# Retention heads of a hybrid encoder block: one transpose for the keys of two heads, and one instruction for the decayed keys

## The chip, the cores and the metric

The kernel runs on one core of a Trainium2 chip. The metric is device time in microseconds of one execution, the median of the runs shown. The engines are TensorE (PE for its matmuls, PEld for its weight loads), VectorE (DVE), ScalarE (ACT), GpSimd (POOL) and SyncE (SP, which only starts transfers here).

## The reference, cut to what matters

One layer: a norm and modulation of x (1024 tokens by 1024 columns), one wide input projection, a retention branch of 8 heads and a latent-attention branch of 8 heads, and an output projection. The change lies in the retention branch. There q and k (64 columns per head) get a rotary embedding, and each direction works in chunks of 128 tokens:

```
scores = einsum('bhnik,bhnjk->bhnij', qc, kc) * decay_intra
intra  = einsum('bhnij,bhnjv->bhniv', scores, vc)
kv_chunk = einsum('bhnjk,bhnjv->bhnkv', kc * k_decay, vc)
state' = state * chunk_decay + kv_chunk
cross  = einsum('bhnik,bhnkv->bhniv', qc * q_decay, states)
```

The output is intra + cross, forward with the diagonal and backward without it, summed.

## The kernel before, in words

Everything is float32. The large projections are made of three products of rounded halves (wh, wl, hh, hl), which is why lines 65 to 67 (the helper mm3) hold most of the matmuls. Weights come in pages (wpage, line 86, loaded by SP), which ACT rounds (line 80) and POOL subtracts (line 81).

The retention stage is a loop over four groups g of two heads. Within a group it runs over eight chunks t of 128 tokens. For each chunk: 24 matmuls project q, k and v into a PSUM bank of the tag acc (four banks; the tag sm has the other four). For group 0 these projections are already done. ACT copies v (line 345). DVE multiplies q and k by cosine and sine (lines 354 and 356), POOL subtracts and adds into the even slots of a buffer of eight slots of 64 columns (lines 360 and 361): q of head 0, q of head 1, k of head 0 and k of head 1 in slots 0, 2, 4 and 6. DVE copies the two q into slots 1 and 3 (line 362). Slots 5 and 7 hold zeros that line 328 put there once. DVE makes the decayed keys kd with four small instructions (line 366), one per head and direction. TensorE transposes the buffer in four blocks of 128 columns (line 370): q0 q0, q1 q1, k0 and zeros, k1 and zeros. ACT copies all four blocks to qkT (line 372), DVE makes the decayed q (line 374), TensorE the scores of both heads (line 378, where the zero half silences the second copy of q), DVE the masked scores (line 380), and TensorE the products of kd and v (line 385), which go into the states ST (lines 389 to 399).

After its eight chunks a group computes its output gates sg (line 414), the outputs in two halves (lines 424 and 425), their norm (lines 430 to 437), transposes (line 442) and the product ro (line 444), which SP writes to memory (line 446). After the four groups, mla_gate runs for two groups of gates of the other branch (line 460). Its results stand in buffers of the tag qkT until ACT's queue has written them to memory (line 461).

The order on each engine is not that of the text. A planner with a cost model orders the instructions of each engine ahead of the run, so the matmuls of lines 65 to 67 of the group's gates and of the next group stand between the small matmuls of a chunk. On the chip each engine then takes its instructions in that fixed order.

Of the kernel before, what the change touches and what calls it, by code (L numbers as in the profile page):

```python
# [9 lines left out]
F32 = mybir.dt.float32  # L10
# [3 lines left out]
ALU = mybir.AluOpType  # L14
# [4 lines left out]
P = 128  # L19
# [11 lines left out]
def body(tc, I, O):  # L31
# [292 lines left out]
    mgD = dram.tile([H, P, S], F32, name="mgD")  # L324

    rbuf = [p_ret.tile([P, 8, 64], F32, name=f"rb{i}", tag=f"rb{i}") for i in range(2)]
    for b_ in rbuf:
        G.memset(b_, 0.0)

    for g in range(4):  # L330
        w = w0 if g == 0 else [wpage(I["w_ret"][g][j], 1024, 2) for j in range(4)]
        vv = []
        ST = p_ret.tile([P, NT, 2, P], F32, name="ST", tag="ST")
        sT = [None] * NT
        qdT = [None] * NT
        for t in range(NT):
            if g == 0 and t < NB0:
                ps = acc0[t]
            else:
                ps = acc()  # L340
                for k in range(KT):
                    wh, wl = w[k // 2]
                    mm3(ps, hh[k][:, ts_(t)], hl[k][:, ts_(t)], wh[:, k % 2], wl[:, k % 2], k == 0, k == KT - 1)
            v_ = p_ret.tile([P, 2, P], F32, name="v", tag="v", bufs=9)
            A.copy(out=v_.rearrange("p h d -> p (h d)"), in_=ps[:, 256:512])  # L345
            vv.append(v_)
            xq = ps[:, 0:256]
            if g == 0 and NACC <= t < NB0:
                xq = p_ret.tile([P, 256], F32, name="xq", tag="o", bufs=5)
                A.copy(out=xq, in_=ps[:, 0:256])  # L350
            xq = xq.rearrange("p (a d) -> p a d", d=32)
            t1 = p_ret.tile([P, 4, 2, 32], F32, name="t1", tag="t1", bufs=2)
            t2 = p_ret.tile([P, 4, 2, 32], F32, name="t2", tag="t2", bufs=2)
            V.tensor_tensor(out=t1.rearrange("p a b d -> p (a b) d"), in0=xq,
                            in1=Cr[:, t:t + 1].broadcast_to([P, 8, 32]), op=ALU.mult)
            V.tensor_tensor(out=t2.rearrange("p a b d -> p (a b) d"), in0=xq,
                            in1=Sr[:, t:t + 1].broadcast_to([P, 8, 32]), op=ALU.mult)
            r_ = rbuf[t % 2]
            rv = r_.rearrange("p (a z) d -> p a z d", z=2)[:, :, 0].rearrange("p a (b d) -> p a b d", b=2)
            G.tensor_tensor(out=rv[:, :, 0], in0=t1[:, :, 0], in1=t2[:, :, 1], op=ALU.subtract)  # L360
            G.tensor_tensor(out=rv[:, :, 1], in0=t1[:, :, 1], in1=t2[:, :, 0], op=ALU.add)
            V.tensor_copy(out=r_[:, 1:4:2], in_=r_[:, 0:4:2])
            kd = p_ret.tile([P, 2, 2, 64], F32, name="kd", tag="kd", bufs=2)
            for h in range(2):
                for d in range(2):
                    V.tensor_scalar(out=kd[:, h, d], in0=r_[:, 4 + 2 * h],
                                    scalar1=kfac[:, 2 * g + h, d:d + 1], scalar2=None, op0=ALU.mult)
            tp = sm(512)
            for a in range(4):
                T.transpose(tp[:, ts_(a)], r_[:, 2 * a:2 * a + 2].rearrange("p a b -> p (a b)"), ident)  # L370
            qkT_ = p_ret.tile([P, 4, P], F32, name="qkT", tag="qkT", bufs=2)
            A.copy(out=qkT_.rearrange("p a b -> p (a b)"), in_=tp)
            qdT_ = p_ret.tile([P, 2, P], F32, name="qdT", tag="qdT", bufs=8)
            V.tensor_tensor(out=qdT_, in0=tp[:, 0:256].rearrange("p (a b) -> p a b", a=2),
                            in1=qfac[:, 2 * g:2 * g + 2], op=ALU.mult)
            scp = sm(256)
            for h in range(2):
                T.matmul(scp[:, ts_(h)], qkT_[:, 2 + h], qkT_[:, h], start=True, stop=True)
            sT_ = p_ret.tile([P, 2, P], F32, name="sT", tag="sT", bufs=8)
            V.tensor_tensor(out=sT_, in0=scp.rearrange("p (h d) -> p h d", h=2), in1=mask[:, 2 * g:2 * g + 2],  # L380
                            op=ALU.mult)
            sT[t], qdT[t] = sT_, qdT_
            kv = sm(256)
            for h in range(2):
                T.matmul(kv[:, ts_(h)], kd[:, h].rearrange("p a b -> p (a b)"), v_[:, h], start=True, stop=True)
            kvv = kv.rearrange("p (h d) -> p h d", h=2)
            if t < NT - 1:
                if t == 0:
                    V.tensor_copy(out=ST[0:64, 1], in_=kvv[0:64])
                else:  # L390
                    for h in range(2):
                        V.scalar_tensor_tensor(out=ST[0:64, t + 1, h], in0=ST[0:64, t, h],
                                               scalar=gch[0:64, 2 * g + h:2 * g + h + 1], in1=kvv[0:64, h],
                                               op0=ALU.mult, op1=ALU.add)
            if t > 0:
                A.copy(out=ST[64:128, t - 1], in_=kvv[64:128])
        for t in range(NT - 2, 0, -1):
            for h in range(2):
                V.scalar_tensor_tensor(out=ST[64:128, t - 1, h], in0=ST[64:128, t, h],
                                       scalar=gch[64:128, 2 * g + h:2 * g + h + 1], in1=ST[64:128, t - 1, h],  # L400
                                       op0=ALU.mult, op1=ALU.add)


        wg = [wpage(I["w_rg"][g][j], 1024, 4) for j in range(2)]
        sg = p_ret.tile([P, 2, S], F32, name="sg", tag="sg")
        for h in range(2):
            for half in range(2):
                ps = acc()
                for k in range(KT):
                    wh, wl = wg[k // 4]  # L410
                    rh = hh[k][:, half * 512:half * 512 + 512]
                    rl = hl[k][:, half * 512:half * 512 + 512]
                    mm3(ps, wh[:, k % 4, ts_(h)], wl[:, k % 4, ts_(h)], rh, rl, k == 0, k == KT - 1)
                A.activation(sg[:, h, half * 512:half * 512 + 512], ps, AF.Silu)

        for half in range(2):
            mv = p_ret.tile([P, 4, 2, 2], F32, name="mv", tag="mv", bufs=2)
            ob = []
            for q in range(4):
                t = half * 4 + q  # L420
                op = sm(256)
                lo, hi = (64, 128) if t == 0 else (0, 64) if t == NT - 1 else (0, 128)
                for h in range(2):
                    T.matmul(op[:, ts_(h)], sT[t][:, h], vv[t][:, h], start=True, stop=False)  # L424
                    T.matmul(op[:, ts_(h)], qdT[t][lo:hi, h], ST[lo:hi, t, h], start=False, stop=True)  # L425
                o_ = p_ret.tile([P, 2, P], F32, name="o", tag="o", bufs=5)
                A.copy(out=o_.rearrange("p h d -> p (h d)"), in_=op)
                for h in range(2):
                    bs = p_ret.tile([P, 6], F32, name="bs", tag="bs", bufs=4)
                    V.bn_stats(out=bs, in_=o_[:, h])  # L430
                    V.bn_aggr(out=mv[:, q, h], in_=bs)
                ob.append(o_)
            rst = p_ret.tile([P, 4, 2], F32, name="rst", tag="rst", bufs=2)
            rstd(rst.rearrange("p a b -> p (a b)"), mv[:, :, :, 1].rearrange("p a b -> p (a b)"), 8)
            for q in range(4):
                for h in range(2):
                    V.tensor_scalar(out=ob[q][:, h], in0=ob[q][:, h], scalar1=mv[:, q, h, 0:1],
                                    scalar2=rst[:, q, h:h + 1], op0=ALU.subtract, op1=ALU.mult)
            for h in range(2):
                tp = sm()  # L440
                for q in range(4):
                    T.transpose(tp[:, ts_(q)], ob[q][:, h], ident)
                ro = p_ret.tile([P, 512], F32, name="ro", tag="ro", bufs=2)
                V.scalar_tensor_tensor(out=ro, in0=tp, scalar=gnw[:, 2 * g + h:2 * g + h + 1],
                                       in1=sg[:, h, half * 512:half * 512 + 512], op0=ALU.mult, op1=ALU.mult)
                SY.dma_start(out=retD[2 * g + h, :, half * 512:half * 512 + 512], in_=ro)
# [14 lines left out]
                A.dma_start(out=mgD[2 * n + h, :, sl], in_=mo)  # L461

    for n in range(MG0):
        mla_gate(n, p_ret, "qkT")
    rts.close()


# [498 lines left out]
```

## Time and profile before

| | |
|---|---|
| median of 3 runs | 1058.83 us (1058.5 to 1059.71) |
| profiled execution, its time | 1057.49 us |
| its span, from the first to the last instruction | 1055.3 us |
| mean granted clock of TensorE | 0.988 of full speed |

The span is what the views of the trace divide up. The profiled execution lies 1.34 us under the median, so differences are taken within the trace and then applied to the median.

### The profile page before, as it was taken

The numbers are of one execution on the slowest core, as the hardware profiler recorded it, in microseconds if no ns is written. First come the engines' busy times: TensorE is split into PE (matmuls) and PEld (weight loads), VectorE is DVE, ScalarE is ACT, GpSimd is POOL, SyncE is SP. The second block draws the span as 40 slices with busy tenths as digits, with TensorE's granted clock in tenths as the row PEclk, the third lists the DMA queues.
The fourth block names the chain that finished last, engine by engine and source line by source line (L and its number), as shares of the span: only waits on it lengthen the run. The fifth ranks groups of instructions, "written<-read, shape, count | busy, mean of one in ns | idle before, by whom it ended". The sixth has DMA issues, their size and how long they took to land.

```text
span 1055.3 us, 15223 instructions
## 1 busy us (share of the span) xinstructions
PE 1018.1 (96%) x5736; PEld 888.3 (84%) x5736; DVE 581.4 (55%) x1390; ACT 426.0 (40%) x800; POOL 404.1 (38%) x311
## 2 busy tenths in 40 slices
PE   5899999999999999999999999989999999989998
PEld 4687887888888888998888889879889999878887
DVE  7996546444643534336302116777877777883342
ACT  6654213312321322124322006577767776772100
POOL 2233315213411411224633217943466555873210
PEclk8899999999999999999999999999999999998999
DMA  9721103101110212224654520100000000003522
GB/s 365 264 64 57 41 1 120 41 2 62 63 36 20 85 47 73 102 84 136 201 171 153 183 85 11 41 1 2 20 21 21 2 20 22 21 20 120 169 101 70
DMA packets 30744, 82.27 MB, mean 78 GB/s; under 512 B 3536, under 2 KB 4560, under 8 KB 30672
## 3 DMA queue, kind: packets, MB, share of 16 engines
q1 hardware_dynamic: 25920, 72.92, 20.4%
q10 hardware_dynamic: 4752, 8.39, 2.2%
q8 instruction: 45, 0.74, 0.3%
q14 instruction: 27, 0.22, 0.1%
HBM read 64.52 MB, written 16.78 MB: 77 GB/s over the span
## 4 chain that ended last, share of the span: by engine, by line
PE 82%; DVE 11%; DMA 2%; ACT 2%; issue 2%; POOL 2%; ACTq 0%; DVEq 0%; POOLq 0%
PE acc L65 13%; PE acc L66 13%; PE acc L67 13%; PE pt L739 4%; PE sp L65 4%; PE sp L66 4%; PE sp L67 4%; PE po L66 3%; PE po L67 3%; PE po L65 3%; DVE x L178 2%; DMA wa<-w_ada 2%; PE sm L425 2%; PE sm L424 1%; PE sm L65 1%
## 5 line engine op out<-in xcount | busy, mean ns | idle before, releaser
L81 POOL TENSOR_TENSOR wl<-wr,wh 128x1024 fp32r<-128x1024 f32 (+2 forms) x51 | 115.2, 2268 | 173.2 <-ACT wh L80 148.9
L65 PE MATMUL acc<-wh,hh 128*128 128x512 f32 (+2 forms) x352 | 130.8, 372 | 1.7 <-ACT hh L189 1.7
L66 PE MATMUL acc<-wl,hh 128*128 128x512 f32 (+2 forms) x352 | 130.3, 370 | 0.0
L67 PE MATMUL acc<-wh,hl 128*128 128x512 f32 (+2 forms) x352 | 126.4, 368 | 2.1 <-DVE hl L190 2.1
L725 POOL TENSOR_SCALAR pr<-pr,st 128x1024 f32<-128x1024 f32 x62 | 72.0, 1165 | 101.1 <-DVE st L724 75.5
L65 PE MATMUL acc<-hh,wh 128*128 128x512 f32 x256 | 101.0, 395 | 1.7 <-ACT v L345 1.7
L742 DVE TENSOR_TENSOR pl<-pt,ph 128x512 fp32r<-128x512 f32 x128 | 85.3, 683 | 31.2 <-ACT ph L741 31.1
L66 PE MATMUL acc<-hl,wh 128*128 128x512 f32 x256 | 100.9, 394 | 0.0
L67 PE MATMUL acc<-hh,wl 128*128 128x512 f32 x256 | 100.6, 393 | 0.0
L80 ACT CAST wh<-wr 128x1024 fp32r<-128x1024 f32 (+2 forms) x55 | 53.8, 982 | 104.1 <-PE sm L66 45.1
L741 ACT CAST ph<-pt 128x512 fp32r<-128x512 f32 x128 | 73.1, 591 | 26.6 <-PE pt L739 24.6
L720 DVE TENSOR_REDUCE st<-sp 128x1 f32<-128x1024 f32 x62 | 75.4, 1216 | 6.5 <-PE sp L67 6.4
L66 PE MATMUL po<-pl,vh 128*128 128x256 f32 x256 | 76.5, 299 | 2.1 <-DVE pl L742 2.0
L723 ACT ACTIVATE pr<-sp,st 128x1024 f32<-128x1024 f32 x62 | 69.5, 1121 | 20.8 <-DVE st L721 20.5
L65 PEld LDWEIGHTS acc<-wh,hh 128*128 128x128 f32 x352 | 67.2, 191 | 10.9 <-ACT hh L189 2.1
L67 PEld LDWEIGHTS acc<-wh,hl 128*128 128x128 f32 x352 | 66.0, 188 | 11.1 <-DVE hl L190 3.0
L66 PEld LDWEIGHTS acc<-wl,hh 128*128 128x128 f32 x352 | 67.3, 191 | 8.7
L739 PE MATMUL pt<-ident,pr 128*128 128x128 f32 x496 | 70.2, 274 | 4.0 <-DVE st L724 2.7
L65 PE MATMUL po<-ph,vh 128*128 128x256 f32 x256 | 73.3, 286 | 0.0
L67 PE MATMUL po<-ph,vl 128*128 128x256 f32 x256 | 72.8, 284 | 0.0
L360 POOL TENSOR_TENSOR rb<-t,t 128x128 f32<-128x128 f32 x32 | 14.8, 464 | 135.0 <-PE sm L370 73.4
L739 PEld LDWEIGHTS pt<-ident,pr 128*128 128x128 f32 x496 | 57.9, 141 | 8.5 <-issue 2.9
(353 smaller groups left out, 2474.2 us busy)
## 6 DMA issues: line engine op xcount, KB each, us to landing
x<-w_ada SPq DMA_DIRECT2D x16, 512.0 KB, 7.1
wr<-w_ret SPq DMA_DIRECT2D x16, 512.0 KB, 3.5
wr<-w_rg SPq DMA_DIRECT2D x8, 512.0 KB, 3.5
retD<-ro SPq DMA_DIRECT2D x16, 256.0 KB, 2.1
wr<-w_mg SPq DMA_DIRECT2D x8, 512.0 KB, 3.5
wa<-w_ada SPq DMA_DIRECT2D x8, 512.0 KB, 3.5
wr<-w_out SPq DMA_DIRECT2D x8, 512.0 KB, 4.5
wro<-retD SPq DMA_DIRECT2D x8, 512.0 KB, 3.9
```

The lines of the kernel that those rows point to most:

```text
L65: T.matmul(out, lh, rh, start=first, stop=False, **kw)
L66: T.matmul(out, lh, rl, start=False, stop=False, **kw)
L67: T.matmul(out, ll, rh, start=False, stop=last, **kw)
L80: A.copy(out=hi, in_=raw)
L81: eng.tensor_tensor(out=lo, in0=raw, in1=hi, op=ALU.subtract)
L178: V.scalar_tensor_tensor(out=wa, in0=wa, scalar=1.0, in1=sc, op0=ALU.mult, op1=ALU.mult, accum_out=mp[:, i:i + 1])
L720: V.tensor_reduce(out=st_[:, 0:1], in_=sp, op=ALU.max, axis=AX.X)
L723: A.activation(pr, sp, AF.Exp, bias=st_[:, 1:2], scale=sc_, accum_out=st_[:, 2:3])
L725: G.tensor_scalar(out=pr, in0=pr, scalar1=st_[:, 3:4], scalar2=0.0, op0=ALU.mult, op1=ALU.add)
L739: T.transpose(tp[:, ts_(q)], pr[:, ts_(half * 4 + q)], ident)
L741: A.copy(out=ph[half][:, :, c_], in_=tv)
L742: V.tensor_tensor(out=pl[half][:, :, c_], in0=tv, in1=ph[half][:, :, c_], op=ALU.subtract)
```

## The change

The buffer's zeros go. The copy on line 362 now fills slots 1, 3 and 5, so that slots 5 and 6 hold k0 and k1 side by side. Three blocks are transposed instead of four: q0 q0, q1 q1, and k0 k1 in one. ACT copies the two q blocks to qT, and the k block in two halves of 64 partitions into a buffer kz whose other halves were set to zero once. kz has two copies, which alternate with t. The scores read kz and qT. The four instructions for kd become one product with a broadcast factor. The gates of mla_gate take buffers of the tag ro instead of qkT, which no longer exists.

```diff
-    for b_ in rbuf:
+    kz = [p_ret.tile([P, 2, P], F32, name=f"kz{i}", tag=f"kz{i}") for i in range(2)]
+    for b_ in kz:
         G.memset(b_, 0.0)
...
-            V.tensor_copy(out=r_[:, 1:4:2], in_=r_[:, 0:4:2])
+            V.tensor_copy(out=r_[:, 1:6:2], in_=r_[:, 0:5:2])
             kd = p_ret.tile([P, 2, 2, 64], F32, name="kd", tag="kd", bufs=2)
+            V.tensor_tensor(out=kd, in0=r_[:, 4:7:2].unsqueeze(2).broadcast_to([P, 2, 2, 64]),
+                            in1=kfac[:, 2 * g:2 * g + 2].unsqueeze(3).broadcast_to([P, 2, 2, 64]), op=ALU.mult)
+
+            tp = sm(384)
+            for a, c0 in enumerate((0, 2, 5)):
+                T.transpose(tp[:, ts_(a)], r_[:, c0:c0 + 2].rearrange("p a b -> p (a b)"), ident)
+            qT_ = p_ret.tile([P, 2, P], F32, name="qT", tag="qT", bufs=2)
+            A.copy(out=qT_.rearrange("p a b -> p (a b)"), in_=tp[:, 0:256])
+            kz_ = kz[t % 2]
             for h in range(2):
-                for d in range(2):
-                    V.tensor_scalar(out=kd[:, h, d], in0=r_[:, 4 + 2 * h],
-                                    scalar1=kfac[:, 2 * g + h, d:d + 1], scalar2=None, op0=ALU.mult)
-            tp = sm(512)
-            for a in range(4):
-                T.transpose(tp[:, ts_(a)], r_[:, 2 * a:2 * a + 2].rearrange("p a b -> p (a b)"), ident)
-            qkT_ = p_ret.tile([P, 4, P], F32, name="qkT", tag="qkT", bufs=2)
-            A.copy(out=qkT_.rearrange("p a b -> p (a b)"), in_=tp)
+                A.copy(out=kz_[64 * h:64 * h + 64, h], in_=tp[64 * h:64 * h + 64, 256:384])
...
-                T.matmul(scp[:, ts_(h)], qkT_[:, 2 + h], qkT_[:, h], start=True, stop=True)
+                T.matmul(scp[:, ts_(h)], kz_[:, h], qT_[:, h], start=True, stop=True)
...
-        mla_gate(n, p_ret, "qkT")
+        mla_gate(n, p_ret, "ro")
```

## Rows read from the trace of the kernel before

**Rows 1.** The page: busy time by engine, and the chain that ended last by engine

```profile
PE 1018.1 (96%) x5736; PEld 888.3 (84%) x5736; DVE 581.4 (55%) x1390; ACT 426.0 (40%) x800; POOL 404.1 (38%) x311
...
PE 82%; DVE 11%; DMA 2%; ACT 2%; issue 2%; POOL 2%; ACTq 0%; DVEq 0%; POOLq 0%
```

**Rows 2.** Busy time by stretch, retention: stretch, us, engines' busy us, clock, DMA share, GB/s

```profile
80.00:400.00 320.00, 315.88 (x1686) 268.46 (x1684) 160.42 (x544) 84.50 (x163) 89.96 (x98) 1.00 0.15 47
```

**Rows 3.** What TensorE waited for, 80 to 435 us: total us, times, longest us

```profile
PE acc L65 <- ACT v L345: 1.7, 1, 1.7
PE sm L442 <- DVE o L437: 1.7, 2, 1.4
PE sm L378 <- ACT qkT L372: 0.7, 1, 0.7
```

**Rows 4.** Timeline of one chunk: start us, us, engine, line, operation, count

```profile
380.10 0.60 PE L370 MATMUL sm<-ident,rb 128*128 128x128 f32 x4
...
380.79 0.59 ACT L372 COPY qkT<-sm 128x512 f32<-128x512 f32 x1 [3.29 <-PE sm L370]
...
385.57 0.60 PE L378 MATMUL sm<-qkT 128*128 128x128 f32 x4
```

**Rows 5.** The chain that ended last, in order of time: start us, us, what

```profile
254.47 0.33 PE sm L370 x3
254.80 0.23 PE acc L66
...
380.26 0.44 PE sm L370 x4
```

**Rows 6.** Groups of ACT by line and shape: count, busy us, mean ns, idle before

```profile
L372 ACT COPY qkT<-sm 128x512 f32<-128x512 f32 x32 | 18.8, 587 | 87.3 <-PE sm L370 87.3
...
L396 ACT COPY ST<-sm 64x256 f32<-64x256 f32 x28 | 10.3, 368 | 21.1 <-PE sm L385 16.7 <-DVE ST L392 3.8
L345 ACT COPY v<-acc 128x256 f32<-128x256 f32 x28 | 10.1, 374 | 69.0 <-PE acc L67 37.5 <-PE sm L424 31.4
...
L524 ACT ACTIVATE jk<-acc 128x32 f32<-128x32 f32 x8 | 1.6, 198 | 0.2
```

**Rows 7.** Groups of DVE by line and shape, 80 to 400 us

```profile
L366 DVE TENSOR_SCALAR kd<-rb,kfac 128x64 f32<-128x64 f32 x128 | 45.1, 406 | 0.0
...
L362 DVE COPY rb<-rb 128x128 f32<-128x128 f32 x32 | 7.0, 219 | 1.6 <-POOL rb L361 1.6
```

**Rows 8.** Timeline of single DVE and POOL instructions

```profile
380.82 0.73 DVE L366 TENSOR_SCALAR kd<-rb,kfac 128x64 f32<-128x64 f32 x4
...
431.56 0.42 DVE L482 TENSOR_TENSOR Cq<-Cr,small 128x256 f32<-128x256 f32 x1
431.89 1.66 DVE L482 TENSOR_TENSOR Sq<-Sr,small 128x256 f32<-128x256 f32 x1
...
431.85 1.42 POOL L81 TENSOR_TENSOR wl<-wr,wh 128x576 fp32r<-128x576 f32 x1 [7.89 <-ACT wh L80]
```

**Rows 9.** Timeline between groups 0 and 1

```profile
167.59 2.36 POOL L81 TENSOR_TENSOR wl<-wr,wh 128x1024 fp32r<-128x1024 f32 x1
167.65 4.66 DVE L437 TENSOR_SCALAR o<-o,mv,rst 128x128 f32<-128x128 f32 x8 [2.05 <-POOL rst L62]
...
168.33 0.39 PE L67 MATMUL acc<-wh,hl 128*128 128x512 f32 x1
...
173.69 0.60 PE L370 MATMUL sm<-ident,rb 128*128 128x128 f32 x4
174.96 0.71 PE L378 MATMUL sm<-qkT 128*128 128x128 f32 x4 [0.68 <-ACT qkT L372]
```

**Rows 10.** Timeline of the gates' buffers and of ro, last group

```profile
411.48 0.60 ACT L460 ACTIVATE qkT<-acc 128x512 f32<-128x512 f32 x1 [4.45 <-PE acc L67]
...
413.83 1.41 DVE L444 SCALAR_TENSOR_TENSOR ro<-sm,small,sg 128x512 f32<-128x512 f32 x2 [2.80 <-PE sm L442]
```

**Rows 11.** The gates' tile: issue to landing of its DMA, us, min, median, max

```profile
DMA to landing us min/median/max: 2.0/2.0/3.7
```

## The prediction

> **What bounds the kernel now.** I read the page's busy shares first. TensorE is busy for 96% of the span and holds 82% of the chain that ended last; no other engine passes 55% [rows 1]. A share over the whole span is an average, so next I cut out the stage that the change touches. From 80 to 400 us TensorE is busy for 315.88 of 320 us at its full granted clock (the 2.4 GHz level), while VectorE has 160, ScalarE 85, GpSimd 90 [rows 2]. The idle 4.1 us are explained almost wholly by the list of what TensorE waited for up to 435 us: four waits, 1.7 and 1.7 and 0.7 us by line, and none of them for a weight page [rows 3]. So in this stage an instruction taken from TensorE's stream should be worth its step, and one added on another engine is worth nothing until it makes TensorE wait.
>
> Then I read one chunk. The four transposes start at 380.10, ScalarE copies their result from 380.79 to 381.38, and the scores that read the copy start at 385.57 [rows 4]. In between TensorE runs matmuls of the projections. The reader is to see that the scores come 4.2 us after the copy is done; and that in 32 chunks the scores waited for the copy once [rows 3].
>
> **The change part by part.**
>
> *One transpose of four.* 32 chunks lose one each. The duration shown for a matmul (0.60 for four) overlaps with the next one; the step is what counts, and the chain in order of time gives it: 0.44 us for four, 0.33 for three [rows 5]. So a transpose is 0.11 us, and three in a row are no dearer each than four. 32 x 0.111 = 3.55 us. Because TensorE hardly waits here, all of it is on the path. The lower bound is nothing, if each chunk then waited as long as it had saved; the waits of [rows 3] exclude that as the usual case.
>
> A page weighs against this size. The row's step is 0.11 us [rows 5]. The Trainium skill (TensorE: Matmul & The Clock Gate, Back-to-back issue gap) gives about 81 ns as the sustained spacing of matmuls of 128 columns with their weight loads. By that price 32 of them would give only 2.6 us, an estimate; the row is a duration of the same thing here and decides.
>
> *Copies on ScalarE.* One copy of 128x512 at 0.587 us goes [rows 6]. One of 128x256 comes, at 0.374 as line 345 shows for that shape, and two of 64x128, which no row shows. From 256 to 512 columns a copy grows by 0.213 us, so 128 columns are about 0.374 - 0.107 = 0.267. Half the partitions save nothing: 64x256 took 0.368. Bounds: 0.198 (128x32) and 0.368 (64x256). I take 0.267, because the shape lies between them on the line through the two full copies. A chunk then costs 0.374 + 2 x 0.267 = 0.91 us, 0.32 more than before (bounds 0.18 and 0.52), 10 us more of ScalarE in all. ScalarE is busy for 26% of the stage [rows 2], so this costs nothing as work. As delay, it makes the scores' operands 0.32 us later after transposes that end 0.11 us earlier. The 4.2 us of projection matmuls [rows 4] hide that. Where the cover is gone, the price is visible once: at 173.69 the transposes of a chunk are followed at 174.96 by its own scores, 1.27 us later where four transposes take 0.44, so TensorE lost 0.83 us there [rows 9]. With the change such a spot costs 0.83 + 0.32 = 1.15 us. Behind these copies on ScalarE queue the copy into the states, the copies of v that free a bank, and the rounding of weights; all had their idle time ahead of them [rows 6].
>
> *Decayed keys.* Four instructions take 0.73 us undisturbed [rows 8] and 4 x 0.406 = 1.62 on average with their stalls [rows 7]. One product of 256 elements from two operands in SBUF replaces them; line 482 has the same size and sources and took 0.42, and 1.66 when a GpSimd subtraction of 1.42 us ran at the same time [rows 8]. I take 0.42 for a free one. VectorE gains at least 0.3 us a chunk (10 us in all) and at most 1.2; with such a stall at every chunk it would gain nothing. VectorE is half idle and TensorE doesn't wait for kd, so this is worth nothing by itself.
>
> Here a rule speaks against the change. First the rows: both the old and the new form are stretched when GpSimd works beside them [rows 7, 8]. The Trainium skill (SBUF — State Buffer, Who interferes with whom) says that a VectorE instruction with two SBUF inputs blocks against a GpSimd instruction that reads SBUF, as the paired mode of the old form did. By it the new instruction would keep the stall, and the sum stays as it is; the trace agrees with the 1.66 us.
>
> *The copy on line 362* moves 192 columns instead of 128. It costs 0.219 now [rows 7]; at most it grows in proportion, to 0.33, at least not at all. It lies ahead of the transposes, and the projections between two chunks cover 0.1 us. The zeroing of kz is half as large as that of the buffer and happens before the stage. I cost both at nothing; without that cover the copy is 32 x 0.1 = 3.2 us.
>
> *The gates' buffers.* They now share two buffers with ro. The case nearest to a clash: a gate is made at 411.48 for 0.60 us, its DMA takes 2.0 us to land (once 3.7), so its buffer is free near 414.1, while the next two ro come at 413.83 [rows 10, 11]. The first may take the other buffer and the second comes 0.7 us later. Even at 3.7 VectorE waits some 2 us there, and queued behind that wait are only the statistics of the next outputs, which TensorE covers with the gates' matmuls. I cost this at nothing, at most 2 us once.
>
> *The order.* The planner orders all engines anew from the changed costs. That can't be read from the trace. Its size can be bounded by what a bad spot costs now: from 168.33 to 174.96 TensorE starts one wide matmul and 24 narrow ones, which need 0.23 + 24 x 0.11 = 2.9 us [rows 5, 9], so 3.7 us are lost. The cause shows beside it: a GpSimd subtraction starts at 167.59, and the eight normalizations on VectorE take 4.66 us until its end and beyond, and TensorE's order holds no other matmuls there.
>
> Sum in the profiled execution: 1057.49 - 3.55 = 1053.9. The median of the runs lies 1.34 us higher, so 1058.83 - 3.55 = 1055.3 us, 0.34% less. About 0.2%, 2.1 us, is what a measurement of this kernel can tell from no change.
>
> **The rivals.**
>
> *A. Forecast:* the transposes come off the path and the spots stay as they are. 1055.3, with its own range from 1054.2 to 1056.5, since a chunk or two may meet a short wait. Chance 0.50.
>
> *B. The bad spot goes too.* VectorE reaches the normalizations with less work before them, or the new order puts other matmuls there. For it: the spot hangs on a coincidence of 0.06 us between two engines. Against it: both instructions wait for the same GpSimd result [rows 9], so they start together whenever that order is kept. 1055.3 - 3.7 = 1051.6. Chance 0.13.
>
> *C. The gain is lost again.* The new order opens one more spot of 3.7 us, for instance at another boundary of two groups, where now one of three has one [rows 3]. 1055.3 + 3.7 = 1059.0, no change. For it: the wait at 168 shows how little it takes. Against it: 31 of 32 chunks have no wait of their scores [rows 3], and the other engines are at most half busy [rows 2]. The same time comes if ScalarE's longer copies cost each chunk 0.11 us. Chance 0.20.
>
> *D. Slower: the scores come to stand right behind their copies.* Mechanism: in the new order the projections stand elsewhere, TensorE takes its instructions in order, and a chunk's scores wait for three copies instead of one. Each such chunk costs 1.15 us. It cancels the gain from 3.1 chunks on and is slower by over 2.1 us from (3.55 + 2.1) / 1.15 = 4.9 chunks on. One group of eight: 9.2 - 3.55 = 5.6 us, 1064.5. For it: the second chunk of group 1 is in that state now [rows 9]. Against it: that is one of 32. Chance 0.17.
>
> **How the numbers follow.** A and B are faster, 0.63, of which I leave 0.01 to A's upper end: 0.62. C and that end give 0.21, D 0.17. The likeliest single case is A, so the prediction is 1055.3. For the range I take in B's end (1051.6) and C (1059.0), and D up to five or six chunks, which lies at 1055.3 + 6 x 1.15 = 1062.2; I stop at 1061.5. About 0.05 is left below 1051.2 and about 0.13 above.
>
> **What would show it right or wrong.** Right: 96 transposes of line 370's successor instead of 128, at 0.33 us for three; no new wait of TensorE for kz or qT beyond one or two; the decayed keys near 0.42 us each, longer beside GpSimd; ScalarE's three copies near 0.91 us together. TensorE's idle time between 80 and 435 us then stays near 4 us and the stage ends 3.5 us earlier. Wrong: waits of the scores for kz at many chunks (D), a new gap between two groups (C), or a later stage that lost in its own order what this one gained.

## The result, and the profile after

The changed kernel is slower: 1071.65 us (median of 4 runs, 1070.05 to 1072.52) against 1059.27 us, a ratio of 1.0113, 95% interval 1.0095 to 1.0131. The prediction was 1055.3 us, with a range up to 1061.5.

First the transposes themselves. One chunk of the changed kernel, from the timeline:

```profile
379.86 0.49 PE L370 MATMUL sm<-ident,rb 128*128 128x128 f32 x3
380.44 0.37 ACT L372 COPY qT<-sm 128x256 f32<-128x256 f32 x1 [2.26 <-PE sm L370]
380.71 0.54 ACT L375 COPY kz<-sm 64x128 f32<-64x128 f32 x2
...
385.21 0.60 PE L381 MATMUL sm<-qT,kz 128*128 128x128 f32 x4
```

This answers to [rows 4]: three transposes, three copies that end at 381.25, and the scores 4.0 us later. That part is as forecast. The two groups of ScalarE copies and the two VectorE groups (80 to 400 us), as in [rows 6, 7]:

```profile
L375 ACT COPY kz<-sm 64x128 f32<-64x128 f32 x64 | 16.6, 260 | 0.8
L372 ACT COPY qT<-sm 128x256 f32<-128x256 f32 x32 | 11.9, 373 | 87.8 <-PE sm L370 87.8
```

```profile
L365 DVE TENSOR_TENSOR kd<-rb,kfac 128x256 f32<-128x256 f32 x32 | 23.1, 721 | 0.0
L363 DVE COPY rb<-rb 128x192 f32<-128x192 f32 x32 | 14.9, 467 | 6.1 <-POOL rb L362 6.1
```

The copies cost what was worked out. What changed is TensorE's list of waits, 80 to 435 us, which answers to [rows 3], and its busy time (the first line answers to [rows 2]):

```profile
PE sm L445 <- DVE o L440: 9.5, 5, 3.8
PE acc L65 <- ACT ro L463: 3.5, 1, 3.5
PE acc L65 <- ACT v L346: 2.2, 1, 2.2
PE sm L381 <- ACT kz L375: 0.6, 1, 0.6
```

```profile
80.00:400.00 320.00, 313.46 (x1649) 266.40 (x1648) 148.90 (x448) 87.22 (x223) 93.39 (x98) 0.99 0.14 44
400.00:440.00 40.00, 30.70 (x137) 25.00 (x136) 16.03 (x56) 7.98 (x16) 6.85 (x6) 0.83 0.21 74
...
424.00:430.00 6.00, 5.02 (x12) 3.97 (x13) 0.08 (x1) 2.39 (x4) 0.00 (x0) 0.50 0.45 177
```

Between 400 and 440 us TensorE is idle for 9.3 us, and its mean granted clock is 0.83. The same 40 us had no idle time before:

```profile
400.00:440.00 40.00, 40.00 (x212) 34.53 (x212) 16.33 (x58) 9.12 (x19) 10.29 (x9) 1.00 0.31 106
```

The timeline of the changed kernel shows who is late:

```profile
415.04 0.48 PE L428 MATMUL sm<-ST,qdT 64*128 64x128 f32 x2
...
418.82 2.14 DVE L440 TENSOR_SCALAR o<-o,mv,rst 128x128 f32<-128x128 f32 x8 [2.03 <-POOL rst L62]
...
419.31 2.19 PE L445 MATMUL sm<-ident,o 128*128 128x128 f32 x8 [3.78 <-DVE o L440]
421.33 1.41 DVE L447 SCALAR_TENSOR_TENSOR ro<-sm,small,sg 128x512 f32<-128x512 f32 x2 [0.37 <-PE sm L445]
...
424.33 0.60 ACT L463 ACTIVATE ro<-acc 128x512 f32<-128x512 f32 x1 [8.35 <-DMA retD<-ro]
...
424.98 0.80 PE L65 MATMUL acc<-hh,wh 128*128 128x512 f32 x1 [3.48 <-ACT ro L463]
...
425.46 0.60 ACT L463 ACTIVATE ro<-acc 128x512 f32<-128x512 f32 x1 [0.54 <-ACT ro L463]
...
427.01 0.60 ACT L463 ACTIVATE ro<-acc 128x512 f32<-128x512 f32 x1 [0.95 <-DMA mgD<-ro]
...
428.11 0.60 ACT L463 ACTIVATE ro<-acc 128x512 f32<-128x512 f32 x1 [0.51 <-DMA mgD<-ro]
```

ScalarE's first gate is at 424.33. It waited 8.35 us for the DMA of ro, because the gates now stand in the buffers of ro. It had been at 387.63 before. Until then four finished projections of the gates hold the four acc banks, so no further projection can start: four gates run from 424.33 to 428.71, and none of them waits for TensorE any more. The reader is to see that TensorE waits for the normalized outputs at 419.31 as well. VectorE is not slower there: the eight normalizations take 2.14 us, as they do in the last half before the change. What is missing are the projections that TensorE ran at that time before. In the half before it, where TensorE has no projections left after 406.4 either, two waits of 1.0 and 1.1 us for the normalizations show.

Two landmarks measure the stages: the last transpose of the chunks, and the last of the eight gates (the lines of these instructions: ns, then first and last start). Before:

```profile
L370 PE MATMUL sm<-ident,rb x128: 270/273/288, 85.5 to 386.8; 128*128 128x128 f32 x128
...
L460 ACT ACTIVATE qkT<-acc x8: 592/598/604, 387.6 to 434.4; 128x512 f32<-128x512 f32 x8
```

After:

```profile
L370 PE MATMUL sm<-ident,rb x96: 270/273/421, 86.8 to 386.3; 128*128 128x128 f32 x96
...
L463 ACT ACTIVATE ro<-acc x8: 592/598/600, 424.3 to 449.9; 128x512 f32<-128x512 f32 x8
```

From the last transpose to the last gate it took 434.4 - 386.8 = 47.6 us, and takes 449.9 - 386.3 = 63.6 us: 16.0 us more in the stage between. The chunks themselves end only 0.5 us earlier, where 31 lost transposes should give 3.4; they also start 1.3 us later (86.8 instead of 85.5).

The smaller loss lies between groups 0 and 1, where [rows 9] showed a wait. GpSimd and VectorE there, after:

```profile
165.74 0.21 POOL L61 TENSOR_TENSOR rs_e<-mv,epst 128x8 f32<-128x8 f32 x1 [14.65 <-DVE mv L434]
166.06 2.41 POOL L81 TENSOR_TENSOR wl<-wr,wh 128x1024 fp32r<-128x1024 f32 x1
168.42 1.65 POOL L62 TENSOR_TENSOR rst<-rs_e,neghalf 128x8 f32<-128x8 f32 x1
170.04 2.35 POOL L81 TENSOR_TENSOR wl<-wr,wh 128x1024 fp32r<-128x1024 f32 x1
170.11 4.45 DVE L440 TENSOR_SCALAR o<-o,mv,rst 128x128 f32<-128x128 f32 x8 [4.46 <-POOL rst L62]
```

The new order puts a weight subtraction of 2.41 us between the two small instructions that make rst. The normalizations start at 170.11 instead of 167.65 (the chunks had also started 1.3 us later), and TensorE waits 3.5 us for them instead of 1.4.

### The profile page after: what moved, and what is told of

It reads as the page before. It is cut to its first block, busy times and chain, and to the rows that moved or that the text cites. A ratio compares the mean times of both kernels' runs of the same rounds, so it can differ in the third digit from the quotient of the medians.

```text
span 1069.7 us, 15160 instructions
## 1 busy us (share of the span) xinstructions
PE 1022.3 (96%) x5704; PEld 891.1 (83%) x5704; DVE 569.1 (53%) x1294; ACT 430.4 (40%) x864; POOL 406.6 (38%) x311
## 4 chain that ended last, share of the span: by engine, by line
PE 47%; DVE 3%; ACT 1%; DMA 1%; issue 1%; POOL 1%; ACTq 0%; DVEq 0%; POOLq 0%
PE pt L742 5%; PE acc L65 4%; PE acc L66 4%; PE acc L67 4%; PE sp L65 4%; PE sp L67 4%; PE sp L66 4%; PE po L66 3%; PE po L67 3%; PE po L65 3%; PE sm L67 1%; PE sm L65 1%; PE sm L66 1%; PE pt L655 1%; PE pt L66 1%; PE pt L67 1%
```

## The experiments

Theory G: the gates wait for the last ro, whose buffers they share, and TensorE has no bank for further projections. Rival O: the new instructions and the new order cost the time.

**The gates in buffers of their own.** The changed kernel with the tag qT for the gates, which grows its two buffers to 512 columns. Room comes from the unused eighth slot and from two of the four small statistics buffers.

```diff
-        mla_gate(n, p_ret, "ro")
+        mla_gate(n, p_ret, "qT")
...
-    rbuf = [p_ret.tile([P, 8, 64], ...
+    rbuf = [p_ret.tile([P, 7, 64], ...
...
-                    bs = p_ret.tile([P, 6], F32, name="bs", tag="bs", bufs=4)
+                    bs = p_ret.tile([P, 6], F32, name="bs", tag="bs", bufs=2)
```

> The changed kernel with the gates' results in two buffers of the tag qT instead of ro (room comes from the unused eighth slot of the rotated buffer and two of four tiny statistics buffers). Theory G, the gates wait for the last ro, whose buffers they share, and TensorE runs out of banks for projections: some 15 us of lost TensorE time between 405 and 431 us go away, 1055 to 1060 us. Rival O, the new order and the new instructions on ScalarE and VectorE cost the time: 1068 us or more, as the changed kernel.

1052.89 us, ratio 0.9951 (0.9934 to 0.9968): faster than both kernels, and 18.8 us faster than the changed one. Its landmarks and waits:

```profile
L370 PE MATMUL sm<-ident,rb x96: 270/273/288, 85.7 to 382.9; 128*128 128x128 f32 x96
...
L463 ACT ACTIVATE qT<-acc x8: 592/598/598, 384.1 to 430.5; 128x512 f32<-128x512 f32 x8
```

```profile
PE acc L65 <- ACT v L346: 1.8, 1, 1.8
PE sm L445 <- DVE o L440: 1.5, 2, 1.4
PE sm L381 <- ACT kz L375: 0.6, 1, 0.6
```

From the last transpose to the last gate: 47.6 us, as before the change. The gates are done 3.9 us earlier than before, and the waits are those of [rows 3]. Theory G holds, and O's 1068 us falls. The time is 2 us under the expected range; where these come from was not tried.

**The tag alone.** The kernel before with one word changed.

```diff
-        mla_gate(n, p_ret, "qkT")
+        mla_gate(n, p_ret, "ro")
```

> The kernel before with only the gates' tag changed from qkT to ro. Theory G: slower by about 15 us, 1072 to 1076 us, with ScalarE's first gate waiting for the DMA of ro near 424 us. Rival O: no change, 1058 to 1061 us.

1072.56 us, ratio 1.0135 (1.012 to 1.015): 14.1 us slower, with none of the other edits.

```profile
424.83 0.60 ACT L460 ACTIVATE ro<-acc 128x512 f32<-128x512 f32 x1 [8.45 <-DMA retD<-ro]
```

```profile
L370 PE MATMUL sm<-ident,rb x128: 270/273/290, 85.1 to 386.4; 128*128 128x128 f32 x128
...
L460 ACT ACTIVATE ro<-acc x8: 592/598/598, 424.8 to 450.1; 128x512 f32<-128x512 f32 x8
```

The same wait at the same place, and 450.1 - 386.4 = 63.7 us between the landmarks. This one word is enough for the slowdown, and with the experiment before it is its cause.

**Who asks first.** The changed kernel with the gates' lines ahead of the outputs of group 3, the tag ro kept.

```diff
                 A.activation(sg[:, h, half * 512:half * 512 + 512], ps, AF.Silu)
+        if g == 3:
+            for n in range(MG0):
+                mla_gate(n, p_ret, "ro")
...
-    for n in range(MG0):
-        mla_gate(n, p_ret, "ro")
```

> The changed kernel, tag ro kept, but the gates stand in the text ahead of group 3's outputs, so that they ask for the two ro buffers before the last four ro do. Theory G1, buffers of a tag are given out in the order of the text, so a gate waits until the last ro has its buffer: the 15 us at 405 to 431 us go, 1054 to 1062 us (the outputs may then wait for the gates' DMAs, off TensorE's path). Theory G2, two buffers are too few for both users whoever asks first: 1066 us or more.

1066.88 us, ratio 1.0081 (1.0066 to 1.0097). The gates no longer wait for ro:

```profile
L342 ACT ACTIVATE ro<-acc x8: 591/600/600, 382.6 to 423.3; 128x512 f32<-128x512 f32 x8
```

So with the same two buffers the order of asking decides when the gates run, as G1 says. But the expected time was missed, and by its time alone the run lies in the range of G2, the theory that two buffers are too few whoever asks first. The trace speaks against G2: no engine waits for a buffer of ro, neither for the gates nor for the outputs, and TensorE has no idle time from 400 to 440 us.

```profile
400.00:440.00 40.00, 40.00 (x219) 35.57 (x218) 7.67 (x34) 7.05 (x14) 7.08 (x6) 1.00 0.24 82
```

The time is lost elsewhere. The outputs now come after the gates (their last transposes at 449.7 us, 426.2 in the kernel with the gates' own buffers), and TensorE waits in the next stage for the normalized tiles of the latent branch (400 to 520 us; this wait was 1.8 us before the change):

```profile
PE sm L544 <- DVE cn L535: 6.3, 2, 4.2
```

The spot between groups 0 and 1 was also the long one here (3.5 us). Against the kernel with the gates' own buffers the profiled span is 12.9 us longer (1063.0 and 1050.1); these two account for some 6 us of it, and the rest was not followed up. So the order of the text seems to set more than the buffers, namely what the planner puts first; that was not tried by itself.

**A third buffer.**

```diff
-                ro = p_ret.tile([P, 512], F32, name="ro", tag="ro", bufs=2)
+                ro = p_ret.tile([P, 512], F32, name="ro", tag="ro", bufs=3)
```

> The changed kernel with three buffers of the tag ro instead of two (room from the eighth slot of the rotated buffer and two of four small statistics buffers), the gates still after the last ro in the text. Theory G1: still slow, 1066 to 1073 us, with the first gate near 420 us, after the last outputs. Theory G2: 1054 to 1060 us.

1063.14 us, ratio 1.0049 (1.003 to 1.0068): between the two expectations. The timeline:

```profile
411.53 1.39 DVE L447 SCALAR_TENSOR_TENSOR ro<-sm,small,sg 128x512 f32<-128x512 f32 x2
...
415.04 0.60 ACT L463 ACTIVATE ro<-acc 128x512 f32<-128x512 f32 x1 [0.93 <-DMA retD<-ro]
...
419.40 1.41 DVE L447 SCALAR_TENSOR_TENSOR ro<-sm,small,sg 128x512 f32<-128x512 f32 x2 [0.37 <-PE sm L445]
422.35 0.60 ACT L463 ACTIVATE ro<-acc 128x512 f32<-128x512 f32 x1 [6.71 <-DMA retD<-ro]
```

The first gate comes when the second buffer of the half before is free, and the next only after a ro of the last half is written out. That fits one rule: a freed buffer goes to the next one that asks for it in the order of the text. The last two ro stand ahead of the gates, so they get the third buffer and the first one freed, although they are written 4 us after the first gate. From the last transpose (384.1) to the last gate (442.3) it takes 58.2 us: a third buffer gives back 5.4 of the 16.0.

**The parts alone.** Three transposes, in the kernel before; the second head's keys are left out, and its scores use those of the first.

```diff
-            tp = sm(512)
-            for a in range(4):
+            tp = sm(384)
+            for a in range(3):
...
-                T.matmul(scp[:, ts_(h)], qkT_[:, 2 + h], qkT_[:, h], start=True, stop=True)
+                T.matmul(scp[:, ts_(h)], qkT_[:, 2], qkT_[:, h], start=True, stop=True)
```

> The kernel before with three transposes and a copy of 128x384 per chunk, nothing else; the keys of the second head of each group are left out (its scores use those of the first). The transposes' step alone: 32 x 0.111 = 3.55 us less on TensorE, 1054 to 1057 us, as long as the spot between groups 0 and 1 keeps its size (3.7 us). If the saving does not reach the end: 1058 to 1061 us.

1055.89 us, ratio 0.9974 (0.9965 to 0.9984), which is 1.7 to 3.7 us less.

```profile
L370 PE MATMUL sm<-ident,rb x96: 270/272/299, 85.6 to 382.6; 128*128 128x128 f32 x96
...
L460 ACT ACTIVATE qkT<-acc x8: 592/598/604, 383.3 to 430.2; 128x512 f32<-128x512 f32 x8
```

The transposes end 4.2 us earlier than before, and so do the gates. The saved step reaches the end: 3.8 us between the two profiled spans (1055.3 and 1051.5), 2.3 between the medians.

The decayed keys alone, in the kernel before:

> The kernel before with only the decayed keys in one instruction. Theory G: no effect on the path, 1057 to 1061 us. Rival O in the form that the two-operand instruction collides with GpSimd and delays the normalizations between groups 0 and 1: 1062 us or more, with over 3.5 us of waits of TensorE for the normalized outputs.

1059.55 us, ratio 1.0014 (1.0003 to 1.0025), within G's range. But the spot between groups 0 and 1 took its long form, at the level that O named (waits of TensorE, 80 to 435 us):

```profile
PE sm L440 <- DVE o L435: 3.9, 2, 3.6
```

The last gate of that kernel comes 3.1 us later than before (437.5), and its median is only 1.1 us higher: not all of a wait in this stage reaches the end.

The transposes and copies without the decayed keys, with the gates' own buffers (the first experiment with the four instructions of line 366 put back):

> One transpose for both keys with kz and qT, the four instructions for the decayed keys kept, and the gates in two buffers of the tag qT. Theory G: the 3.55 us of 32 transposes show, 1055 to 1058 us. Rival O in the form that the three copies of ScalarE delay the scores: 1062 us or more, with waits of the scores for kz at many chunks.

1058.41 us, ratio 1.0001 (0.9991 to 1.001). The expected range of G, up to 1058, was missed by little, but nothing of the saving is left: waits elsewhere and a later start ate it.

```profile
PE acc L65 <- ACT v L346: 2.2, 1, 2.2
PE sm L447 <- DVE o L442: 2.0, 1, 2.0
PE acc L65 <- DVE t L357: 1.1, 1, 1.1
PE sm L383 <- ACT kz L377: 0.6, 1, 0.6
```

Not the kz copies (0.6 us once, as against 0.7 for the copies before), but the spot (2.0 instead of 1.4) and two waits for a free bank (3.3 us instead of 1.7). The chunks also start 1.5 us later (87.0 instead of 85.5), for a reason ahead of the retention stage that was not followed up.

**The spot between groups 0 and 1.** The kernel with the gates' own buffers, and the normalizations on ScalarE.

```diff
-                    V.tensor_scalar(out=ob[q][:, h], in0=ob[q][:, h], scalar1=mv[:, q, h, 0:1],
-                                    scalar2=rst[:, q, h:h + 1], op0=ALU.subtract, op1=ALU.mult)
+                    A.activation(ob[q][:, h], ob[q][:, h], AF.Identity, bias=mv[:, q, h, 0:1],
+                                 scale=rst[:, q, h:h + 1])
```

> The changed kernel with the gates' own buffers, and with the eight normalizations of each half on ScalarE instead of VectorE (one small product more on VectorE). If the spot near 168 us comes from GpSimd's subtraction holding up VectorE: the wait of TensorE for the normalized outputs there (1.4 us and its followers) shrinks, 1049 to 1052 us. If it comes from the statistics or from too little other work on TensorE: no gain, 1052 to 1056 us.

1059.72 us, ratio 1.0013 (1.0003 to 1.0022): no gain, worse than the 1052.89 without it, and above both expected ranges. On ScalarE the eight took 3.19 us at 170.62, behind a weight rounding:

```profile
163.71 4.72 POOL L81 TENSOR_TENSOR wl<-wr,wh 128x1024 fp32r<-128x1024 f32 x2 [12.12 <-ACT wh L80]
...
169.59 1.04 ACT L80 CAST wh<-wr 128x1024 fp32r<-128x1024 f32 x1
170.62 3.19 ACT L442 ACTIVATE o<-o,mv,rst 128x128 f32<-128x128 f32 x8
```

They are no longer stretched by GpSimd (3.19 us in the last group too), and TensorE still waits 2.0 us. But rst itself came late here: it was ready at 170.3 us, and at 166.7 in the kernel without this edit. Two weight subtractions stand ahead of it on GpSimd instead of one, and the statistics that it needs ended later too. So the run shows no gain from taking the collision away in this order; what the collision alone costs stays open.

## Why the prediction was wrong

The step that failed is "The gates' buffers ... I cost this at nothing, at most 2 us once". It looked at one near clash and supposed that a gate may take any buffer that is free at the time, so that the gates keep their places. They don't: a buffer goes to those who ask in the order of the text, and the last four ro ask first. The gates move from 387.6 to 424.3, behind the last outputs. Two things were late next that the step didn't count: the acc banks, which four waiting projections hold, and the outputs' own latency, which the gates' matmuls had covered. The step even named these matmuls as the cover ("which TensorE covers with the gates' matmuls"), without asking whether they would still stand there. The term put at nothing, at most 2 us, measured 14.1 us as the tag alone, and 18.8 us as what the changed kernel gains when the gates get buffers of their own. D forecast a slower kernel too, but by another mechanism; none of the rivals was this one.

The transposes were right: 0.11 us each, on the path. Alone they gave 4.2 us at the last gate and 2.3 in the median. With the gates' buffers apart the kernel gains 5.5 us; the forecast gives 3.55 of these to the transposes, and where the other 2 come from is not settled. They don't show at the last gate, which comes at 430.5 us there and at 430.2 with the three transposes alone. The copies were right: 0.373 + 2 x 0.260 = 0.89 us a chunk, against 0.91, hidden by 4.0 us. D, the scores right behind their copies, stayed at one chunk in 32.

The decayed keys and the copy before them were right undisturbed and mis-sized with their stalls. The keys took 0.72 us on average instead of 0.42 (the shortest 0.40, the longest 2.07), a gain of 0.90 a chunk, within the bounds of 0.3 and 1.2. The copy grew from 0.219 to 0.467 us, more than the 0.33 put as the most (the shortest 0.26, the longest 2.43). Together they went from 0.22 + 1.62 to 1.19 us a chunk, a gain of 0.65. The stalls moved in part from the one instruction to the other: with the decayed keys alone changed, the copy ahead of them, the same as before, grew from 0.219 to 0.334 us.

C was right in kind and is a minor part: the spot between groups 0 and 1 grew. In the changed kernel, in that with the gates ahead and in that with the decayed keys alone the longest wait there is about 3.5 us; in the kernel before and in four experiments it is 1.4, in the other two 2.0. In the three kernels with the long wait, and in no other, a weight subtraction stands between lines 61 and 62 on GpSimd. That this order makes the difference was read from the rows and not tried by itself, and what in the change tips the planner is open. It is part of why the parts don't add up: the decayed keys alone give +0.1%, the transposes with their copies 0.0%, and both together -0.5%.

The sum, at the last gate: before 434.4, after 449.9. That is 15.5 later: the stage of outputs and gates takes 16.0 us more, and the chunks end 0.5 us earlier. In the chunks' stage the transposes' 3.4 us were nearly lost to the spot (some 2 us) and to a start 1.3 us later. These two also separate the changed kernel from that with the gates' own buffers, by some 2.1 and 1.1 us, which is 3.2 of the 4.7 between 14.1 and 18.8.

## What to carry to other kernels

When an edit moves a tile to another tag, the question is not whether a buffer is free at that time, but who else asks for that tag earlier in the text, and when the last of them will be done. Work that fills a bottleneck engine's gaps is cover only as long as it can run early, so its buffers must not depend on the work that it covers. And where a planner orders the engines, the same part can be worth different amounts: here the saved transposes came to 0.0 us in one version and 2.3 in another, and a boundary between stages had its short and its long form in versions that differ little. Read the waits of each version before judging the edit.

## What the runs showed of the hardware that was not expected

After the waits of 3.8 and 3.5 us TensorE's granted clock was 0.50 of full speed from 424 to 430 us (the 1.2 GHz level), and matmuls of 512 columns started every 0.43 us instead of 0.23, so the wait cost more than its own length. The Trainium skill (TensorE: Matmul & The Clock Gate, Part 1) describes such a fall to half rate after idle time, and the trace agrees with the level.
